# A hybrid encoder layer in Strassen–Winograd form: matrix memory's rows two tiles ahead, its weights behind the columns, and x's quarter in the fifth operand's buffer

## The chip, the cores and the metric

One core of one Trainium2 chip. The time is the device time of one execution in microseconds (us), and the median of several executions is compared. The span in a profile is the time from the first to the last instruction of one profiled execution.

## What is computed

One layer of a streaming encoder, all in float32: 2048 prompt tokens and 8 x 16 sample tokens, width 1024, so 17 tiles of 128 tokens (16 of the prompt, and the sample batch as tile 16). Four steps:

```python
z = x @ w_in                                  # queries, keys, values, gates, window heads
mix = concat(mlstm(z), window_attention(z))   # group A: 4 heads x 128; group B: 8 heads / 2 kv heads x 64
x = layer_norm(alpha * x + mix @ w_out)
x = layer_norm(alpha * x + (silu(conv(gate)) * conv(value)) @ w_down)   # gate, value: two halves of x @ w_up
```

Group A, the matrix memory, goes tile by tile. With b the running sum of the forget gates' logarithms over a tile, li the input gates', and C, n, m the state from the tile before:

```python
inter = b + m
dmat = where(causal, b[:, None] - b[None, :] + li[None, :], -inf)
mt = maximum(inter, max(dmat, -1))
w_inter = exp(inter - mt)
s = (q @ k.T) * exp(dmat - mt[:, None])
num = w_inter * (q @ C) + s @ v
```

num is divided by the larger of |den| and exp(-mt), normed by head, and C, n and m are carried to the next tile.

## The kernel before

**Phases.** Input projection (four blocks of up to five tiles, `IBLOCKS`), output projection, FFN up, FFN down. Each value is held as two parts, high and low, and each product is three matmuls. The projection works on pairs of halves with seven products instead of eight (Strassen–Winograd): in a block there are five groups g of weight columns, and for each the products s = 1, 7, 6, 2, 5, 3, 4. Their second operands are sums of quarters of x: `x_steps` casts each to high (ACT, L602) and subtracts to low (DVE, L603), into the buffers oh{s} and ol{s} that `x_slot(s)` gives. Beside the products stand direct tiles, ("t", block, tile, part), which multiply a tile of x with the gates' and keys' weights (PE L783). They use quarters of x of their own, hx[b, 1], hx[b, 2], hx[b, "b12"] and hx[b, 3]. So far "b12" lies in oh4/ol4, the fourth product's buffer.

**Banks.** The products of a group write three PSUM banks: A by s = 1 and 2; B by 6, 5 and 3; C by 7 and 4. `i_after` empties them: ACT copies B for s = 6 and 5 (L824 in groups 0 and 1 as scaled copies by `copy`, L816 for a whole bank A or B through `i_out`), DVE adds C to the copy (L828 and L830, for s = 5 and again for s = 4), and between groups ACT copies A to B (L852). A bank can be written again only when its reader is done.

**Order of the work.** PE's order is as the program writes it. `Chains.weave` steps three generators between the products: the sample batch, the matrix memory (`m_chain`) and windowed attention (`a_chain`). Each yields a cost, a delay in estimated time and a count of PSUM banks it needs. On the other engines a scheduler sets the order; `issue_after` holds an instruction behind another, and `behind_pe` holds a DMA behind PE's latest mark. All of the DMAs spoken of here are issued by SP, in SP's order, the weights' loads too: an SP row that waits holds the rows behind it.

**Weights.** A weight unit is loaded (wraw, L477), cast by ACT (L227), and split by DVE (w, L228). Of the input weights some products take sums that the kernel forms itself (txy, zt, and from DRAM zws).

**A tile of matrix memory.** `m_rows` (L1130) takes two transposes on PE (pgr, L1057 and L1058) and makes on DVE rows of 4 x 128: a scan for b (r_b, L1136), li - b (ay, L1137), a second scan for the running maximum (r_M, L1138), the negated row nmrow (L1140, L1141), a further row (L1068) and the carried m (L1144). `m_spread` step 0 writes nmrow to DRAM (zrow, L1150) and step 1 reads it back to all 128 partitions (nm, L1153). `m_tile` then makes columns (pcol on PE, col on DVE, L1079), dt = nm + mask (DVE L1175), emt (ACT L1084), wi = the inter-tile weights (ACT L1187, reads nm), dt's exponentials (ACT L1181), scores weighted by dt (sd, DVE L1198), kw (L1272), then pnum (PE L1282) and the state's update. `m_norm` norms (DVE L1216 to L1227), `m_scaled` makes ms and hn (DVE L1233, ACT L1235), `m_out` transposes hn (pht, PE L1245) and stores.

Before, `m_tile(t)` makes the rows of tile t + 1 right behind its own dt and spreads them in two later steps: step 0 before the scores, step 1 before pnum. So one row set is ahead.

Of the kernel before, what the change touches and what calls it, by code (L numbers as in the profile page):

```python
# [204 lines left out]
class Prog:  # L205
# [373 lines left out]
    def x_steps(self, b, *steps):  # L579

        nc, V = self.nc, self.nc.vector
        r = lambda q: self.xr[b, q]
        for s in steps:
            if s == "t3":
                self.spare = False
                self.xt = e = self.raw_slot([P, 4, HT]) if b else [self.tp.tile([P, 4, HT], F32, name="xt", tag="qk", bufs=2), False]
                V.tensor_sub(e[0], r(4), r(2))
            elif s == "t2":

                V.tensor_add(self.xt[0], self.xt[0], r(1))  # L590
            elif s == "t4":

                V.tensor_sub(r(4), r(3), self.xt[0])
                self.xt[1] = True
            elif s == "t1":

                V.tensor_sub(r(2), r(2), r(1))
            else:
                x = self.xt[0] if s in (7, 6) else r({1: 1, 2: 3, 3: 4, "b12": 2, 5: 2, 4: 4}[s])

                self.hx[b, s] = h, l = self.x_slot(4 if s == "b12" else s)
                nc.scalar.copy(h, x)  # L602
                V.tensor_sub(l, x, h.bitcast(F32))  # L603

# [17 lines left out]
    def i_dense(self):  # L622
# [18 lines left out]
        for q in (2, 4):  # L641
            for _ in range(2 + (q == 2) * 2):
# [15 lines left out]
                 ("t", 0, 0, -1): ["t2", 6], ("t", 0, 2, -1): ["t1", 5, "t4"]}  # L658
        self.sb, self.trans = {}, None

        passages = [{1: ["load"], 7: ["t3", 7], 6: ["t2", 6], 3: [3, "t4"], 4: ["b12", "t1"]},
                    {1: ["load"], 6: ["t3"], 7: [7, "t2"], 5: [6], 3: [3, "t4"], 4: ["b12", "t1"]}]
        sums = 0
        after = None
        for item in self.items:
# [49 lines left out]
            if g == last and b + 1 < nb:  # L715
                if s == 7:
                    self.rope_load(IBLOCKS[b + 1][2], 2)
                for x in passages[b > 0].get(s, ()):
                    if x == "load":
                        self.spare = True  # L720
                        self.x_load(b + 1, 1, 2, 3, 4)
                    else:
                        self.x_steps(b + 1, x)
            if (b, g, s) == (0, last, 4):
                self.x_steps(1, 1, 2)
                after = [6, 1]
            if g == last and b + 1 == nb and s in (7, 5, 2, 3):
                self.x_pair(0, (7, 5, 2, 3).index(s))
            with self.tc.issue_after(behind) if behind and b == 0 else nullcontext():
                self.advance()  # L730
                self.x_steps(0, *begin.get(item, ()))
                if item == ("p", 0, 0, 2):
                    self.x_single(4)
# [87 lines left out]
    def i_after(self, b, g, s):  # L821
# [15 lines left out]
            self.i_out(b, g, 0, 0, A)  # L837
        elif s == 5:
            u4 = self.zev()
            copy(u4, B)  # L840
            add(u4)
            self.i_out(b, g, 1, 1, u4)
        elif s == 4:
            add(self.u2)
            self.i_out(b, g, 1, 0, self.u2)
# [235 lines left out]

    def m_emt(self, col):
        emt = self.work("emt", [P, MH], bufs=2)
        self.nc.scalar.activation(emt, col[:, 36:40], AF.Exp)  # L1084
        return emt

    def place(self, t, blocks=IBLOCKS):
# [8 lines left out]
    def m_chain(self):  # L1096
# [3 lines left out]
        pend = None  # L1100
        self.rows = {}
        there = lambda t: t < NPT and self.i_done > self.place(t)[0]
        for t in range(NPT):
            while not there(t):
                yield 0, 500
            if pend is None:
                self.m_rows(t)
                self.m_spread(t, 0)
                self.m_spread(t, 1)
# [4 lines left out]
            hn = self.m_norm(*(yield from self.m_tile(t, *pend, *self.rows.pop(t))))  # L1114
            pend = None
            yield 950, 3000, 1
            self.m_scaled(hn)
            if there(t + 1):
                if t + 1 not in self.rows:
                    self.m_rows(t + 1)  # L1120
                    self.m_spread(t + 1, 0)
                    self.m_spread(t + 1, 1)
                pend = self.m_load(t + 1, *self.place(t + 1)),
            yield 150, 6800, 1
            self.m_out(t, hn[0])
            self.chains.done["m"] = t
        nc.sync.dma_start(self.a["m_p"], self.mc)
        nc.sync.dma_start(self.a["cn_p"], self.C)

    def m_rows(self, t):  # L1130
# [14 lines left out]
        self.rows[t] = [i, nm]  # L1145

    def m_spread(self, t, step):
        nc, z = self.nc, self.zrow[t]
        if step == 0:
            self.behind_pe(nc.sync.dma_start(z.rearrange("o (h m) -> (o h) m", h=MH), self.rows[t][1]))  # L1150
            return
        self.rows[t][1] = nm = self.work("nm", [P, MH, 129], bufs=2)
        self.behind_pe(nc.sync.dma_start(nm.rearrange("p h m -> p (h m)"), z.to_broadcast([P, MH * 129])))  # L1153

    def m_load(self, t, b, ti):
# [95 lines left out]
    def m_tile(self, t, load, i, nm):  # L1251
# [3 lines left out]
        col = self.m_cols(i)  # L1255
        with self.tc.issue_after(self.colcopy.ins):
            dt = self.m_masked(nm[:, :, :P], self.mcau)
        ahead = t + 1 < NPT and self.i_done > self.place(t + 1)[0]
        if ahead:
            self.m_rows(t + 1)  # L1260
        yield 330, 2800
        emt = self.m_emt(col)
        wi = self.m_inter(nm)
        self.m_exps(dt, col)
        yield 0, 5000, 2
        if ahead:
            self.m_spread(t + 1, 0)
        ps = self.m_scores(qk)
        kt = self.m_ktok(qk)
        sd = self.m_weighted(ps, dt)  # L1270
# [956 lines left out]
```

## Time and profile before

| | |
|---|---|
| median of 3 runs | 2307.58 us (2306.45 to 2310.1) |
| the profiled execution: its time | 2307.89 us |
| its span | 2305.7 us |
| PE, busy | 2266.6 us |
| DVE, busy | 1808.2 us |
| ACT, busy | 1306.8 us |
| POOL, busy | 225.5 us |

PE is TensorE's matmuls, PEld its weight loads, which overlap them; DVE is VectorE, ACT ScalarE, POOL GpSimd, SP SyncE (SPq where it issues a DMA). Times in views are us from the start of the span. A row of the timeline gives start, duration, engine, line, operation, written and read buffers, shapes, and in brackets how long the engine stood idle before it and what ended that. The input projection with matrix memory and attention between its products takes the first 870 us or so; the matrix memory's first prompt tile starts at about 280 us.

### The profile page before, as it was taken

The page shows a single profiled execution, that of the slowest core. Times are in us where ns is not written, and L with a number is a line of the kernel's source. Part 1 is how long each engine was busy: PE and PEld are TensorE (multiplying, and loading weights), DVE is VectorE, ACT ScalarE, POOL GpSimd, SP SyncE. Part 2 cuts the span into 40 slices and gives each one's busy share as a digit, 9 for nine tenths or more (in the row PEclk, how much of TensorE's full clock was granted, in tenths as well). Part 3 has the DMA queues.
Part 4 walks back from the last instruction along what each step waited for, and adds up shares of the span by engine and source line. Part 5 has one row for each costly group of instructions (what it writes and reads, how often), then busy time and mean ns, then how long its engine had stood idle before and what let it go on. Part 6 is the DMA issues. An engine that isn't in the chain of part 4 may idle for free.

```text
span 2305.7 us, 39752 instructions
## 1 busy us (share of the span) xinstructions
PE 2266.6 (98%) x14329; PEld 2086.1 (90%) x14329; DVE 1808.2 (78%) x3157; ACT 1306.8 (57%) x2465; POOL 225.5 (10%) x289
## 2 busy tenths in 40 slices
PE   8999999999999999999999999999999999999998
PEld 8999989898887778999999999999999988888887
DVE  8777686787789888987788666778766787796897
ACT  5453466676765665555556455555554644654753
POOL 0001001101122121200002000002000000000100
PEclk9999999999999999999999999999999999999999
DMA  7898999899986767787777889888998786656753
GB/s 279 299 322 287 297 308 328 295 303 332 320 278 237 241 220 248 282 322 282 275 270 263 282 309 322 308 305 270 328 292 260 240 286 225 240 196 225 242 188 110
DMA packets 299797, 629.23 MB, mean 273 GB/s; under 512 B 47373, under 2 KB 140625, under 8 KB 299601
## 3 DMA queue, kind: packets, MB, share of 16 engines
q1 hardware_dynamic: 298736, 623.55, 79.1%
q10 hardware_dynamic: 864, 3.15, 0.4%
q8 instruction: 113, 1.85, 0.3%
q14 instruction: 84, 0.68, 0.1%
HBM read 456.01 MB, written 170.59 MB: 272 GB/s over the span
## 4 chain that ended last, share of the span: by engine, by line
PE 78%; DVE 10%; DMA 6%; ACT 3%; issue 2%; SPq 0%; POOL 0%; DVEq 0%; ACTq 0%; POOLq 0%
PE dps L1931 18%; PE fup L1931 18%; PE dps L758 11%; PE dps L2135 6%; PE fht L2135 6%; PE fup L2135 5%; PE dps L232 2%; PE dps L233 2%; PE dps L234 2%; DMA txy<-wdn 2%; DVE w L228 2%; PE dps L783 1%; DMA w<-zws 1%; PE psx L767 1%; PE ppo L1420 1%
## 5 line engine op out<-in xcount | busy, mean ns | idle before, releaser
L1931 PE MATMUL dps<-hh,uw 128*128 128x384 f32 (+1 forms) x1848 | 477.5, 327 | 5.4 <-DVE u L1964 2.6
L1931 PE MATMUL fup<-hh,uw 128*128 128x384 f32 (+1 forms) x1848 | 476.4, 326 | 0.0
L1979 DVE SCALAR_TENSOR_TENSOR cc<-u,cw,cc 128x768 f32<-128x768 f32 (+1 forms) x264 | 257.7, 978 | 125.0 <-ACT cc L1977 121.6
L1931 PEld LDWEIGHTS dps<-hh,uw 128*128 128x128 f32 x1848 | 329.2, 188 | 7.9 <-DVE u L1964 3.2
L1931 PEld LDWEIGHTS fup<-hh,uw 128*128 128x128 f32 x1848 | 329.3, 188 | 0.0
L1931 PE MATMUL fup<-hl,uw 128*128 128x384 f32 (+1 forms) x924 | 301.3, 326 | 0.2 <-DVE hl L228 0.2
L1931 PE MATMUL dps<-hl,uw 128*128 128x384 f32 (+1 forms) x924 | 301.0, 326 | 0.0
L758 PE MATMUL dps<-w,oh 128*128 128x256 f32 x1344 | 252.1, 283 | 4.6 <-DMA w<-zws 2.2
L758 PEld LDWEIGHTS dps<-w,oh 128*128 128x128 f32 x1344 | 210.1, 188 | 17.1 <-issue 9.3
L228 DVE TENSOR_TENSOR w<-wraw,w 128x1024 fp32r<-128x1024 f32 (+1 forms) x155 | 185.8, 1202 | 50.4 <-ACT w L227 48.0
L227 ACT CAST uw<-wraw 128x1024 fp32r<-128x1024 f32 x126 | 123.2, 981 | 173.4 <-PE dps L2135 104.1
L227 ACT CAST w<-wraw 128x1024 fp32r<-128x1024 f32 (+1 forms) x155 | 155.0, 1005 | 88.9 <-PE dps L758 44.3
L228 DVE TENSOR_TENSOR uw<-wraw,uw 128x1024 fp32r<-128x1024 f32 x126 | 142.5, 1131 | 63.9 <-ACT uw L227 63.8
L758 PE MATMUL dps<-w,ol 128*128 128x256 f32 x672 | 187.2, 279 | 0.0
L1977 ACT ACTIVATE cc<-u,cw 128x768 f32<-128x768 f32 (+1 forms) x132 | 131.9, 1000 | 95.6 <-DVE u L1973 92.6
L758 PE MATMUL dps<-oh,w 128*128 128x256 f32 x896 | 167.0, 282 | 7.8 <-ACT zev L824 3.9
L1931 PEld LDWEIGHTS fup<-hl,uw 128*128 128x128 f32 x924 | 173.5, 188 | 1.1 <-DVE hl L228 1.1
L1931 PEld LDWEIGHTS dps<-hl,uw 128*128 128x128 f32 x924 | 173.5, 188 | 0.0
L2135 PE MATMUL fup<-uw,fu 128*128 128x512 f32 x726 | 169.3, 389 | 0.1
L2135 PEld LDWEIGHTS fup<-uw,fu 128*128 128x128 f32 x726 | 136.1, 188 | 28.7 <-ACT fht L2142 0.5
L2135 PE MATMUL dps<-uw,fu 128*128 128x512 f32 x660 | 160.9, 389 | 0.1
L758 PEld LDWEIGHTS dps<-oh,w 128*128 128x128 f32 x896 | 139.7, 188 | 14.1 <-ACT zev L824 4.5
(346 smaller groups left out, 4563.6 us busy)
## 6 DMA issues: line engine op xcount, KB each, us to landing
uw<-zw SPq DMA_DIRECT2D x176, 512.0 KB
zw<-uw SPq DMA_DIRECT2D x88, 512.0 KB
w<-zws SPq DMA_DIRECT2D x72, 512.0 KB
wv<-wup SPq DMA_DIRECT2D x66, 512.0 KB
wraw<-wi SPq DMA_DIRECT2D x62, 512.0 KB
wraw<-zt SPq DMA_DIRECT2D x60, 512.0 KB
wraw<-wdn SPq DMA_DIRECT2D x45, 512.0 KB
wraw<-wo SPq DMA_DIRECT2D x40, 512.0 KB
```

The lines of the kernel that those rows point to most:

```text
L227: nc.scalar.copy(hi, src)
L228: nc.vector.tensor_sub(lo, src, hi.bitcast(F32))
L232: mm(out, ah, bh, start=start, stop=False)
L233: mm(out, ah, bl, start=False, stop=False)
L234: self.mark = mm(out, al, bh, start=False, stop=stop)
L758: self.mark = mm(o, l, r, start=s in (1, 7) and c == k == i == 0, stop=k == 3 and i == 2, skip_group_check=True)
L767: mm(o, x[:, k], w[:, k], start=s == 1 and k == i == 0, stop=s in (2, 4) and k == 3 and i == 2, skip_group_check=True)
L783: mm(o, x, w, start=k == i == 0, stop=k == KD - 1 and i == 2, skip_group_check=True)
L1931: mm(ps, l[:, k], r[:, k], start=s in (1, 7) and k == 0 and i == 0, stop=k == 3 and i == 2, skip_group_check=True)
L1977: S.activation(c[:, v], u[:, v, 2:2 + n], AF.Identity, bias=w[3], scale=w[2])
L1979: V.scalar_tensor_tensor(c[:, v], u[:, v, i:i + n], w[i], c[:, v], op0=ALU.mult, op1=ALU.add)
L2135: mm(ps, l[:, k, c], r[:, k], start=s in (1, 4, 7) and u == 0 and k == 0 and i == 0, stop=u == nu - 1 and k == n - 1 and i == 2, skip_grou ...
```

## The change

Three things, in the diff below.

1. x's quarter "b12" goes to oh5/ol5 for blocks 1 to 3. For block 1 it is cast after product s = 5 of block 0's last group, behind the copy of bank B (`i_after` now returns that instruction), not after s = 4.
2. Matrix memory's rows: `m_tile(t)` no longer makes rows. Behind `m_scaled(t)` and the load of tile t + 1, the rows of tile t + 2 are made; step 0 of their spread follows `m_out(t)`; step 1 stands in `m_tile(t + 1)` behind its exponentials. A third entry in `self.rows` says whether step 1 has been issued. Where rows are missing, `at_once` makes them with both steps. Tile 0's and tile 1's rows are made this way: tile 0's when it starts, tile 1's behind `m_scaled(0)`. The first yield in `m_tile` goes from 330 to 180.
3. wi is issued behind emt.

```diff
-                self.hx[b, s] = h, l = self.x_slot(4 if s == "b12" else s)
+                self.hx[b, s] = h, l = self.x_slot((5 if b else 4) if s == "b12" else s)
...
-        passages = [{1: ["load"], 7: ["t3", 7], 6: ["t2", 6], 3: [3, "t4"], 4: ["b12", "t1"]},
+        passages = [{1: ["load"], 7: ["t3", 7], 6: ["t2", 6], 5: ["b12"], 3: [3, "t4"], 4: ["t1"]},
...
-                        self.x_steps(b + 1, x)
+                        with self.tc.issue_after(behind) if x == "b12" and s == 5 else nullcontext():
+                            self.x_steps(b + 1, x)
...
-            with self.tc.issue_after(behind) if behind and b == 0 else nullcontext():
+            with self.tc.issue_after(behind) if behind and b == 0 and s == 1 else nullcontext():
...
-            copy(u4, B)
+            done = copy(u4, B).ins
             add(u4)
             self.i_out(b, g, 1, 1, u4)
+            return done
...
-        self.nc.scalar.activation(emt, col[:, 36:40], AF.Exp)
+        self.emtcopy = self.nc.scalar.activation(emt, col[:, 36:40], AF.Exp)
...
+        def at_once(t):
+            if t not in self.rows:
+                self.m_rows(t)
+                self.m_spread(t, 0)
+                self.m_spread(t, 1)
...
             self.m_scaled(hn)
             if there(t + 1):
-                if t + 1 not in self.rows:
-                    self.m_rows(t + 1)
-                    self.m_spread(t + 1, 0)
-                    self.m_spread(t + 1, 1)
+                at_once(t + 1)
                 pend = self.m_load(t + 1, *self.place(t + 1)),
+            ahead = there(t + 2) and t + 2 not in self.rows
+            if ahead:
+                self.m_rows(t + 2)
             yield 150, 6800, 1
             self.m_out(t, hn[0])
+            if ahead:
+                self.m_spread(t + 2, 0)
...
-        ahead = t + 1 < NPT and self.i_done > self.place(t + 1)[0]
-        if ahead:
-            self.m_rows(t + 1)
-        yield 330, 2800
+        yield 180, 2800
         emt = self.m_emt(col)
-        wi = self.m_inter(nm)
+        with self.tc.issue_after(self.emtcopy.ins):
+            wi = self.m_inter(nm)
         self.m_exps(dt, col)
+        if t + 1 in self.rows and not self.rows[t + 1][2]:
+            self.m_spread(t + 1, 1)
         yield 0, 5000, 2
-        if ahead:
-            self.m_spread(t + 1, 0)
...
-        if ahead:
-            self.m_spread(t + 1, 1)
```

Lines of the changed kernel are 1 to 8 higher: L824 becomes L825, L828 and L830 become L829 and L831, L1079 becomes L1081, L1150 and L1153 become L1158 and L1161, L1175 becomes L1183, L1375 becomes L1379.

The instructions move at three places. First, ACT at the end of block 0's last group: the copy of bank B for s = 5 (L824), the gates' weights (128x2x264), the copy for s = 3 (L816), and the casts of x (L602). Before:

```order
L824 COPY zev<-dps 128x512
L227 CAST w<-wraw 128x2x264 x2
L816 COPY zev<-dps 128x512
L602 CAST oh<-xr 128x1024
L227 CAST w<-wraw 128x1024
L602 CAST oh<-xr 128x1024
L227 CAST w<-wraw 128x1024
```

Now:

```order
L825 COPY zev<-dps 128x512
L602 CAST oh<-xr 128x1024
L227 CAST w<-wraw 128x2x264 x2
L817 COPY zev<-dps 128x512
L602 CAST oh<-xr 128x1024
L227 CAST w<-wraw 128x1024 x2
```

The quarter's cast, before the last L602 of the piece, is now the first, ahead of three weight casts.

Second, DVE at the end of block 1's last group, where tile 0 of the matrix memory starts. Before (col, dt, the scan of tile 1's rows, the addition that empties bank C, and the subtraction of tile 1's rows):

```order
L1079 COPY col<-pcol 128x36
L1175 TENSOR_TENSOR dt<-nm,k_mcau 128x512
L1136 SCALAR_TENSOR_TENSOR r_b<-pgr,k_seg 4x128
L830 TENSOR_TENSOR zev<-dps,zev 128x512
L1137 TENSOR_TENSOR ay_765<-pgr,r_b 4x128
```

Now:

```order
L1081 COPY col<-pcol 128x36
L831 TENSOR_TENSOR zev<-dps,zev 128x512
L603 TENSOR_TENSOR ol<-xr,oh 128x1024
L1183 TENSOR_TENSOR dt<-nm,k_mcau 128x512
L228 TENSOR_TENSOR w<-wraw,w 128x1024
```

The addition has come ahead of dt, and tile 1's rows are gone from here.

Third, tile 1 of the matrix memory. SP before, from the write of tile 1's row (zrow_73) to its broadcast:

```order
L1150 DMA zrow_73<-nmrow 4x129
L929 DMA ropet<-rope 128x192
L1302 DMA kva<-zkv_161 128x256
L577 DMA xr<-xq 128x1024
L909 DMA zt<-txy 128x1024
L477 DMA wraw<-zws_2_94 128x1024
L477 DMA wraw<-wi 128x1024
L1153 DMA nm<-zrow_73 128x516
```

Now, with tile 0's output (zmix from mixm) and tile 2's row (zrow_74) behind it:

```order
L1158 DMA zrow_73<-nmrow 4x129
L910 DMA zt<-txy 128x1024
L477 DMA wraw<-wi 128x1024
L1161 DMA nm<-zrow_73 128x516
L477 DMA wraw<-zws_3_95 128x1024
L1247 DMA zmix_176<-mixm 128x4x128
L1158 DMA zrow_74<-nmrow 4x129
```

Two rows stand between the write and the broadcast where six stood, and both have moved behind the norm of tile 0. On DVE the same tile, before (the last addition of a group's bank C, a weight's split, col, dt and the scan of tile 2's rows):

```order
L1380 TENSOR_TENSOR aes<-k_sink,amx 128x4
L828 SCALAR_TENSOR_TENSOR zev<-dps,zev 128x512
L228 TENSOR_TENSOR w<-wraw,w 128x1024
L1079 COPY col<-pcol 128x36
L1175 TENSOR_TENSOR dt<-nm,k_mcau 128x512
L1136 SCALAR_TENSOR_TENSOR r_b<-pgr,k_seg 4x128
```

Now (L1379 are the four reductions of attention, two rows each, of which the first is shown):

```order
L228 TENSOR_TENSOR w<-wraw,w 128x1024
L1081 COPY col<-pcol 128x36
L1183 TENSOR_TENSOR dt<-nm,k_mcau 128x512
L1379 ISA sc,amx<-psc,k_mswa 128x256
L1379 ISA amx 128x1
...
L829 SCALAR_TENSOR_TENSOR zev<-dps,zev 128x512
L1383 SCALAR_TENSOR_TENSOR amx<-amx,nsink 128x4
L228 TENSOR_TENSOR w<-wraw,w 128x1024
```

dt, with the wait for nm, has come ahead of the four reductions and of the addition that empties bank C. The rows of tile 1 and of tile 2 stand further up, the scan, the subtraction and the second scan of tile 1 between the small instructions of tile 0's norm ahead of ms:

```order
L1231 TENSOR_TENSOR mr<-mr,emt 128x4
L1144 SCALAR_TENSOR_TENSOR r_b<-pgr,k_seg 4x128
L1232 RECIPROCAL mr<-mr 128x4
L906 TENSOR_TENSOR txy<-txy 128x512
L1233 TENSOR_TENSOR mq<-bmv,mr 128x4
L1145 TENSOR_TENSOR ay_765<-pgr,r_b 4x128
L1234 TENSOR_TENSOR mq<-mq,mr 128x4
L907 TENSOR_TENSOR txy<-txy 128x512
L1235 TENSOR_SCALAR mq<-mq 128x4
L1146 SCALAR_TENSOR_TENSOR r_M<-k_seg,mc,ay_765 4x128
L1241 TENSOR_TENSOR ms<-ms,mr 128x4
```

More of the change, by code (lines that the diff above doesn't have):

```diff
@@ L1106, in m_chain @@
             if pend is None:
-                self.m_rows(t)
-                self.m_spread(t, 0)
-                self.m_spread(t, 1)
+                at_once(t)
                 pend = self.m_load(t, *self.place(t)),
@@ L1113, in m_chain @@
                 yield 0, 1000, 2
-            hn = self.m_norm(*(yield from self.m_tile(t, *pend, *self.rows.pop(t))))
+            hn = self.m_norm(*(yield from self.m_tile(t, *pend, *self.rows.pop(t)[:2])))
             pend = None
@@ L1144, in m_rows @@
         V.tensor_add(self.mc, bc[:, P - 1:P], M[:, P - 1:P])
-        self.rows[t] = [i, nm]
+        self.rows[t] = [i, nm, False]
     def m_spread(self, t, step):
@@ L1151, in m_spread @@
             return
-        self.rows[t][1] = nm = self.work("nm", [P, MH, 129], bufs=2)
+        self.rows[t][1:] = nm, _ = self.work("nm", [P, MH, 129], bufs=2), True
         self.behind_pe(nc.sync.dma_start(nm.rearrange("p h m -> p (h m)"), z.to_broadcast([P, MH * 129])))
```

## The prediction, made before the result was seen

> **What bounds the kernel now.** I first read the page's table of busy times, then the busy time of the engines in three stretches of the span up to the two FFN halves (start and end; length; busy time of PE, PE's weight loads, DVE, ACT, POOL; granted clock; DMA share; GB/s).
>
> ```profile
> PE 2266.6 (98%) x14329; PEld 2086.1 (90%) x14329; DVE 1808.2 (78%) x3157; ACT 1306.8 (57%) x2465; POOL 225.5 (10%) x289
> 0.00:290.00 290.00, 279.22 (x2409) 270.15 (x2410) 215.04 (x347) 140.43 (x226) 13.73 (x17) 1.00 0.86 297
> 290.00:470.00 180.00, 169.47 (x1409) 156.78 (x1409) 137.38 (x399) 123.14 (x318) 16.82 (x17) 0.99 0.92 310
> 470.00:870.00 400.00, 396.32 (x2663) 329.24 (x2662) 328.37 (x931) 265.04 (x697) 72.72 (x56) 1.00 0.82 273
> ```
>
> PE is the bound: it works 2266.6 of 2305.7 us, so a change that leaves its matmuls alone can win at most the 39.1 us in which it stands. The edits act between about 145 and 870 us. From 290 to 470 (matrix memory's tiles 0 to 3) PE stands 10.5 us, from 470 to 870 only 3.7. Which waits those are, the view of waits tells (who waits for whom: total us, times, longest).
>
> ```profile
> PE dps L758 <- ACT zev L824: 4.4, 4, 2.5
> PE dps L783 <- DVE zev L830: 2.8, 2, 2.1
> PE dps L783 <- DVE ol L603: 2.7, 1, 2.7
> PE dps L758 <- DMA w<-zws: 2.2, 5, 0.8
> PE dps L758 <- ACT zev L816: 0.9, 1, 0.9
> PE pnum L1282 <- DVE sd L1198: 0.9, 1, 0.9
> PE pgr L1057 <- ACT pth L1415: 0.8, 1, 0.8
> PE pht L1245 <- ACT hn L1235: 1.7, 2, 1.0
> ```
>
> I then went to each in the timeline. The profiled execution took 2307.89 us, 2.2 more than its span; the median of the runs shown is 2307.58, so I sum against 2307.89 and take off 0.3 at the end.
>
> **The change part by part. x's quarter.** Timeline of ACT, DVE and PE before the first direct tile of block 1 (start, us, engine, line; in brackets the idle time before it and what ended it).
>
> ```profile
> 145.23 0.58 ACT L824 COPY zev<-dps 128x512 f32<-128x512 f32 x1
> 147.47 0.64 ACT L227 CAST w<-wraw 128x528 fp32r<-128x528 f32 x1 [0.51 <-DMA wraw<-wg]
> 151.53 1.05 ACT L227 CAST w<-wraw 128x1024 fp32r<-128x1024 f32 x1 [0.82 <-DMA wraw<-wi]
> 152.48 1.04 ACT L602 CAST oh<-xr 128x1024 fp32r<-128x1024 f32 x1
> 155.49 1.21 DVE L603 TENSOR_TENSOR ol<-xr,oh 128x1024 fp32r<-128x1024 f32 x1
> 153.57 0.39 PE L783 MATMUL dps<-w,oh 128*128 128x264 f32 x1 [0.28 <-ACT oh L602]
> 156.75 0.40 PE L783 MATMUL dps<-w,ol 128*128 128x264 f32 x1 [2.67 <-DVE ol L603]
> ```
>
> The quarter's cast stands behind a weight's cast that waits for its DMA, and behind the last product on the fourth operand. PE wants the quarter at about 153.3 and stands 0.28 for the high half and 2.67 for the low one. After the change the cast is the row behind the copy L824, which ends at 145.81. With its 1.04 and DVE's 1.21, behind at most one weight split, both halves are ready by about 149.3, four microseconds early. The move puts 1.04 us of ACT ahead of the gates' last weight cast at 147.47, which then ends at 149.2, four microseconds ahead of PE too: nothing new is late there, and PE's product hides it; without that cover it would cost its 1.04. Term: **-3.0**, with 0 and -3.0 as its ends, since what PE gains it may give to the next weights.
>
> **Rows of tile 1 no longer ahead of a column group's end.** Around tile 0 on DVE and PE:
>
> ```profile
> 289.54 0.68 DVE L1175 TENSOR_TENSOR dt<-nm,k_mcau 128x512 f32<-128x512 f32 x1
> 290.14 0.40 DVE L1136 TENSOR_TENSOR_SCAN r_b<-pgr,k_seg 4x128 f32<-4x128 f32 x1
> 290.47 0.65 DVE L830 TENSOR_TENSOR zev<-dps,zev 128x512 f32<-128x512 f32 x1
> 291.18 0.51 PE L783 MATMUL dps<-w,oh 128*128 128x264 f32 x2 [0.71 <-DVE zev L830]
> ```
>
> In the new order the addition stands straight behind col, with dt behind it and no scan: over 1 us earlier, so the 0.71 goes: **-0.7**. The scans of tile 1 go from this place, which is where DVE is short before sd: of the 0.9 that pnum waits I take **-0.5** (ends 0 and -0.9). The A copy's wait of 0.9 (L816, at 323) goes with the same backlog: **-0.9** (ends 0 and -0.9).
>
> **wi behind emt.** The largest wait left is 2.55 us at 327:
>
> ```profile
> 320.39 0.38 SPq L1153 DMA_DIRECT2D nm<-zrow  x1
> 325.97 1.28 ACT L1187 ACTIVATE wi<-nm 128x128 f32<-128x128 f32 x4 [2.87 <-DMA nm<-zrow]
> 327.16 1.03 ACT L227 CAST w<-wraw 128x1024 fp32r<-128x1024 f32 x1
> 328.33 1.28 ACT L1235 ACTIVATE hn<-hn,ms 128x128 f32<-128x128 f32 x4
> 329.52 0.58 ACT L824 ACTIVATE zev<-dps 128x512 f32<-128x512 f32 x1
> 330.14 0.39 PE L758 MATMUL dps<-oh,w 128*128 128x256 f32 x1 [2.55 <-ACT zev L824]
> ```
>
> wi of tile 1, which nobody needs yet, waits at the head of ACT for the broadcast, and the copy that frees a PE bank stands behind it. Behind emt it stands some 12 us later, so at this place ACT's 2.87 of idle and 1.28 of work go and the copy is done in time: **-2.5** (ends -1.3, where hn holds the copy, and -2.55).
>
> **The wait that is added.** Tile 1 is not two ahead. Its rows are made and spread at once when tile 0 is normed; only tiles 2 to 15 are made earlier. That moves nm of tile 1 from 320 to behind ms, and the consumer on DVE, dt, stands where it stood. The prices come from these rows: the seven DVE instructions of one row set at tile 0 (first and last), the SP pair, ms and the next consumers.
>
> ```profile
> 280.08 0.41 DVE L1136 TENSOR_TENSOR_SCAN r_b<-pgr,k_seg 4x128 f32<-4x128 f32 x1
> 282.08 0.14 DVE L1141 COPY nmrow<-mc 4x1 f32<-4x1 f32 x1
> 281.58 0.28 SPq L1150 DMA_DIRECT2D zrow<-nmrow  x1
> 284.78 0.32 SPq L1153 DMA_DIRECT2D nm<-zrow  x1
> 328.14 0.15 DVE L1233 TENSOR_TENSOR ms<-ms,mr 128x4 f32<-128x4 f32 x1
> 334.20 0.60 PE L1245 MATMUL pht<-ident,hn 128*128 128x128 f32 x4
> 336.56 0.41 DVE L1375 CUSTOM_DVE_ANT_0 sc<-psc,k_mswa 128x256 f32<-128x256 f32 x1
> ```
>
> From ms on: the row set interleaved with an addition and a weight split is done 2.8 us later; issue 0.3; landing up to 3.2 (281.58 to 284.78, SP standing meanwhile, with weight loads queued behind it); the broadcast 5.6 (320.39 to 325.97). So nm lands at ms + 11.9. Then dt (0.7 by the row at 289.54), four reductions of 0.41 that overlap (about 1.4 in all) and the addition L828 (0.6, as the one at 290.47), which in the new order all stand behind dt: the bank C is free at ms + 14.6. By the new PE order C is wanted 8.0 us of matmuls behind pht. The rows have pht 5.9 behind ms's end, of which 2.5 is the wait that goes, so 3.4: wanted at ms + 11.4, and PE stands 3.2 us. If pht follows as soon as hn is done (ms + 1.4), it is 5.2. I take **+3.5**, near the first; the ends are 0 (if ms comes early against PE) and +5.2. Queued behind the waiting dt on DVE are those reductions, the addition and a weight split; behind wi, which waits on ACT for the same nm, are dt's exponentials and a weight cast. PE waits for all of these.
>
> Whether the clock pays as well, one place shows:
>
> ```profile
> 457.00:462.40 5.40, 3.31 (x28) 3.10 (x27) 5.37 (x9) 5.40 (x16) 0.00 (x0) 1.00 0.94 269
> 462.40:466.00 3.60, 3.60 (x20) 3.60 (x19) 3.60 (x6) 2.70 (x9) 0.00 (x0) 0.53 1.04 333
> ```
>
> Behind the wait of 2.1 us there the granted clock was 0.53 for 3.6 us, which costs 1.7 us; behind the 2.67 and the 2.55 above I see no such stretch. One of three: an end of +1.7 for the range, not a term. (The Trainium skill, "TensorE: Matmul & The Clock Gate", section "What's actually happening", has the clock fall after an idle window of about 3.4 us; the drop behind 2.1 us disagrees. By that rule the new wait would cost nothing more below 3.4 us and 1.7 above.)
>
> **Tiles 2 to 15 and the rest.** The row sets are as many as before (16 of about 2.1 us of DVE, 280.08 to 282.22) and only stand elsewhere; their broadcasts start a tile earlier, so ACT no longer waits for nm. PE barely stood behind those waits: from 470 to 870 its whole idle time is 3.7. I take **-0.8**, the pgr row's wait (ends 0 and -2). The weights (2.2), the wait of 2.1 and its clock I leave: the addition there still stands behind tile 4's work on DVE.
>
> Sum: -3.0 - 0.7 - 0.5 - 0.9 - 2.5 - 0.8 + 3.5 = -4.9; 2307.89 - 4.9 - 0.3 = **2302.7**. The forecast's own range, with the ends of its terms, is 2299.5 to 2306.5.
>
> **Rivals.** *The new wait is hidden.* If zrow lands in under 1 us, or dt comes late on DVE anyway, the +3.5 goes: 2299.2. For it: ACT and DVE are each under 77% busy from 290 to 470. Against it: the SP pair above took 3.2 and 5.6 us, at a DMA share of 0.92. (The Trainium skill, "DMA: Bandwidth & Descriptors", section "Anatomy of one DMA — SWDGE (gpsimd) path", gives about 2.0 us plus bytes over 436 GB/s for a transfer. An estimate by it is 2.0 and 2.6 for this pair, 4.2 us under the rows, which would hide the wait; the rows disagree.) Chance 0.17.
>
> *x's gain is eaten by the weights behind it.* Block 1's first products follow at once.
>
> ```profile
> 161.58 1.23 DVE L228 TENSOR_TENSOR w<-wraw,w 128x1024 fp32r<-128x1024 f32 x1
> 167.77 0.39 PE L758 MATMUL dps<-oh,w 128*128 128x256 f32 x2
> ```
>
> The weights ready at 162.81 are used at 167.88, with PE 3 us earlier at 164.9: 2.1 us to spare, so this pair holds; but from 184 on products are fed at a DMA share near 0.9, and five waits for w<-zws show where none is spare. All of it lost: 2305.7. Chance 0.18.
>
> *The change does little:* tile 1 waits as long as it gains and x too is eaten, or the scheduler's order hides both: about 2307. Chance 0.05.
>
> *Slower: the rows stand ahead of ms.* In the new order the scan, the subtraction and the second scan of a row set stand on DVE between the norm's small instructions (the scan is 0.41 by its row; of the set's 2.1 I take 1.2 for these three), so ms, hn and pht come that much later at each of 14 tiles. It decides where pht follows hn on PE by less than 1.2 us; two places wait already (1.7 us). At tile 0 the slack is 4.6 (hn ends 329.6, pht starts 334.2). With ten tiles without slack it costs 12.0: 2314.7, and it takes eight or nine to be slower by over 0.2% than before. Chance 0.15.
>
> **How the numbers follow.** Forecast 0.45. About 0.2% (4.6 us) is what a measurement of this kernel can tell from no change, so faster is under 2303.0. The forecast lies on that line: 0.22 faster, 0.23 same. With the hidden wait (0.17), faster is 0.39 in all, rounded to 0.40. Same: 0.23, 0.18 for the eaten gain, 0.05 for little, less rounding 0.45. Slower 0.15. The range 2297 to 2311 takes in the hidden wait with 2 us more at tiles 2 to 15, the eaten gain, the clock's 1.7, and half of the slower case.
>
> **What would show it.** In the changed profile: the wait for ol L603 at 154 gone and the ACT cast of x before 148; no wait at 290 and 327; a wait of PE of some 3 us about 10 us behind the first pht, ended by the addition (now L829), with DVE's dt waiting for nm; no ACT wait for nm at tiles 2 to 15; the pht waits as they were. I am wrong if the pht waits grow, if waits for w<-zws grow by as much as x gained, or if PE's idle time from 470 to 870 moves by over 2 us.

## The result, and the profile after

The changed kernel took 2306.29 us, median of 22 runs (2299.81 to 2309.52), beside 2309.77 of the kernel before in 22 runs of the same sessions (2306.22 to 2320.71). The ratio is 0.9984, 95% interval 0.9978 to 0.9990: 3.7 us less, between 2.3 and 5.1. The forecast was a ratio of 0.9979, just inside that interval. The profiled execution has a span of 2303.8 us, 1.9 under that of before.

The same three stretches of the span in the changed kernel (columns as in the prediction):

```profile
0.00:290.00 290.00, 282.39 (x2435) 273.50 (x2436) 219.50 (x352) 142.59 (x230) 13.66 (x17) 1.00 0.86 300
290.00:470.00 180.00, 168.27 (x1401) 156.78 (x1400) 138.58 (x421) 120.06 (x320) 20.49 (x19) 0.98 0.92 314
470.00:870.00 400.00, 395.69 (x2656) 329.90 (x2655) 321.81 (x911) 265.04 (x694) 71.73 (x55) 1.00 0.81 272
```

PE has 3.2 us more work in the first 290 us: it stands less there, which is x's quarter. From 290 to 470 it stands 11.7 us, 1.2 more than before, and the granted clock is lower (0.98). The part on matrix memory has won nothing there. PE's waits in the whole of the changed kernel, those of the projection that answer to the rows of before, and the new ones:

```profile
PE dps L784 <- DVE zev L831: 4.7, 2, 4.4
PE dps L759 <- ACT zev L825: 2.5, 3, 1.5
PE pgr L1059 <- DVE C L1297: 1.7, 1, 1.7
PE dps L759 <- DVE zev L831: 1.7, 1, 1.7
PE dps L759 <- DMA w<-zws: 1.7, 3, 0.7
PE pnum L1286 <- DVE sd L1206: 1.3, 1, 1.3
PE dps L759 <- ACT dps L854: 1.3, 1, 1.3
PE ppt L1418 <- ACT pth L1419: 0.9, 1, 0.9
PE pht L1253 <- ACT hn L1243: 0.8, 1, 0.8
PE pht L1253 <- ACT pth L1419: 0.7, 1, 0.7
PE dps L759 <- ACT zev L817: 0.4, 1, 0.4
```

The wait of 2.7 for ol (L603 at the direct tile) is gone, and so is the one of 2.55 for a copy at 327. In their place are one of 4.4 for an addition (2.1 before), one of 1.7 for the pgr row, one of 1.5 for another copy (at 499), one of 1.3 for the bank's copy L854 and one of 0.9 for pth. The 1.7 for another addition, at 575, cannot be put down to the change: it was 0.85 in the first profile of the kernel before and 1.69 in its second one.

**x's quarter.** ACT, DVE and PE of the changed kernel before block 1's first direct tile:

```profile
145.00 0.58 ACT L825 COPY zev<-dps 128x512 f32<-128x512 f32 x1
145.48 1.05 ACT L602 CAST oh<-xr 128x1024 fp32r<-128x1024 f32 x1
147.37 0.63 ACT L227 CAST w<-wraw 128x528 fp32r<-128x528 f32 x1 [0.31 <-DMA wraw<-wg]
146.56 1.23 DVE L603 TENSOR_TENSOR ol<-xr,oh 128x1024 fp32r<-128x1024 f32 x1
152.84 0.41 PE L784 MATMUL dps<-w,oh 128*128 128x264 f32 x2
153.09 0.28 PE L784 MATMUL dps<-w,ol 128*128 128x264 f32 x1
```

Both halves are there at 147.8, five us before PE uses them, and the gates' last weights are cast at 148.0, when they were before. PE starts with the low half 0.25 us behind the high one. Counted by the same matmul in both traces, PE is 0.2 us ahead at 150 us and 3.7 ahead from 158 to 230.

**The end of block 2.** There PE is 3.9 us ahead at 451 us (by the matmul that starts at 451.0 in before) and 0.8 behind at 464. Not all of that is standing: counted from 100 us on, PE has done 12 more of the chains' matmuls than before at the first of these points and 24 more at the second. DVE and PE of the changed kernel, and the clock:

```profile
455.62 1.23 DVE L228 TENSOR_TENSOR w<-wraw,w 128x1024 fp32r<-128x1024 f32 x1
456.77 1.12 DVE L1297 SCALAR_TENSOR_TENSOR C<-C,wi,pcu 128x129 f32<-128x129 f32 x4
458.94 0.83 DVE L1230 SCALAR_TENSOR_TENSOR hn<-pnum,bmv,og 128x128 f32<-128x128 f32 x3
459.84 0.66 DVE L831 TENSOR_TENSOR zev<-dps,zev 128x512 f32<-128x512 f32 x1
455.92 0.28 PE L784 MATMUL dps<-w,ol 128*128 128x264 f32 x1
460.56 0.81 PE L784 MATMUL dps<-w,oh 128*128 128x264 f32 x2 [4.36 <-DVE zev L831]
```

```profile
456.00:460.70 4.70, 0.34 (x3) 0.14 (x1) 4.70 (x21) 2.79 (x8) 0.00 (x0) 0.90 0.90 283
460.70:464.00 3.30, 3.30 (x15) 3.30 (x16) 2.83 (x8) 1.64 (x4) 1.72 (x1) 0.50 0.99 302
464.00:468.00 4.00, 4.00 (x26) 4.00 (x25) 2.32 (x3) 1.82 (x4) 0.19 (x1) 0.67 1.00 360
```

The addition that empties bank C ends at 460.5, as it ended at 461.0 before, though PE needs it at 456.2. The state update and the norm of a matrix memory tile stand ahead of it on DVE; in the order of before they did not. The wait of 4.4 is followed by half clock from 459.8 to 466.6 us; the last of the three stretches takes in a part at full clock.

### The profile page after: what moved, and what is told of

Same layout as the page of the kernel before. It is cut to its first block, busy times and chain, and to the rows that moved or that the text cites. A ratio compares the mean times of both kernels' runs of the same rounds, so it can differ in the third digit from the quotient of the medians.

```text
span 2303.8 us, 39754 instructions
## 1 busy us (share of the span) xinstructions
PE 2265.1 (98%) x14329; PEld 2088.1 (91%) x14329; DVE 1804.9 (78%) x3157; ACT 1305.4 (57%) x2465; POOL 227.5 (10%) x289
## 3 DMA queue, kind: packets, MB, share of 16 engines
q8 instruction: 113, 1.85, 0.3%
## 4 chain that ended last, share of the span: by engine, by line
PE 82%; DVE 7%; DMA 5%; issue 3%; ACT 2%; POOL 0%; SPq 0%; DVEq 0%; ACTq 0%; POOLq 0%
PE dps L1935 19%; PE fup L1935 19%; PE dps L759 11%; PE dps L2139 6%; PE fht L2139 6%; PE fup L2139 5%; PE dps L232 2%; PE dps L233 2%; PE dps L234 2%; DVE w L228 1%; PE dps L784 1%; PE ppo L1424 1%; DMA w<-zws 1%; PE psx L768 1%; PE psc L1375 1%
```

## The experiments

A ratio is to the runs of the kernel before on the same chip, with its interval; in us, times 2310. PE's idle time is given in two pieces of work, cut at the same matmuls in every trace: those that start at 140, 285 and 880 us in before, so that the pieces hold the same projection work, and all of the matrix memory's work is done at the last cut. It is the length of the piece less PE's busy time. Each profile is of one execution, and those of x alone and of the change with the sums later are of the fastest of their 12 runs, so the idle times go with the profile and not with the median. The rows for the second piece (length; busy of PE, PE's weight loads, DVE, ACT and POOL; clock; DMA share; GB/s) of before, of the change, of x alone and of the rows without the hold on wi:

```profile
285.06:880.05 594.99, 580.78 (x4153) 498.85 (x4152) 478.52 (x1350) 395.06 (x1026) 92.43 (x75) 1.00 0.85 285
```

```profile
281.23:877.46 596.23, 579.84 (x4153) 500.72 (x4152) 472.45 (x1348) 392.95 (x1025) 92.93 (x75) 0.99 0.84 285
```

```profile
280.70:873.29 592.59, 580.89 (x4153) 499.56 (x4153) 476.48 (x1348) 395.30 (x1027) 92.09 (x75) 1.00 0.85 286
```

```profile
281.21:887.99 606.78, 581.71 (x4153) 500.85 (x4152) 471.87 (x1348) 393.99 (x1027) 90.43 (x74) 0.99 0.83 280
```

| kernel | ratio to before | us | idle, first piece | idle, second piece | its length |
|---|---|---|---|---|---|
| before; again | 1 | 0 | 4.2; 3.6 | 14.2; 14.5 | 595.0; 596.6 |
| the change; again | 0.9984 (0.9978 to 0.9990) | -3.7 | 1.2; 1.6 | 16.4; 17.6 | 596.2; 599.2 |
| x alone | 0.9977 (0.9967 to 0.9988) | -5.3 | 0.3 | 11.7 | 592.6 |
| rows and wi | 1.0015 (1.0006 to 1.0024) | +3.5 | 3.8 | 20.4 | 603.2 |
| wi alone | 1.0005 (0.9994 to 1.0016) | +1.2 | 3.5 | 14.4 | 597.4 |
| x and wi | 0.9983 (0.9971 to 0.9995) | -3.9 | 0.8 | 14.9 | 597.5 |
| the change, tile 1 ahead | 0.9988 (0.9977 to 0.9999) | -2.8 | 0.4 | 16.8 | 597.4 |
| the change, chains held | 0.9994 (0.9982 to 1.0006) | -1.4 | 0.6 | 17.2 | 596.7 |
| the change, sums later | 0.9983 (0.9973 to 0.9993) | -3.9 | 0.7 | 13.1 | 593.4 |
| x alone, sums later | 0.9969 (0.9958 to 0.9981) | -7.2 | 0.8 | 11.2 | 591.2 |
| x and rows, no hold | 1.0032 (1.0018 to 1.0046) | +7.4 | 1.1 | 25.1 | 606.8 |
| x alone, chains held | 0.9985 (0.9974 to 0.9996) | -3.5 | 0.7 | 17.6 | 600.5 |

**x's quarter alone**, on the kernel before (the lines on `done` and on `s == 1` in the diff of the change belong to it):

```diff
-                self.hx[b, s] = h, l = self.x_slot(4 if s == "b12" else s)
+                self.hx[b, s] = h, l = self.x_slot((5 if b else 4) if s == "b12" else s)
...
-        passages = [{1: ["load"], 7: ["t3", 7], 6: ["t2", 6], 3: [3, "t4"], 4: ["b12", "t1"]},
+        passages = [{1: ["load"], 7: ["t3", 7], 6: ["t2", 6], 5: ["b12"], 3: [3, "t4"], 4: ["t1"]},
...
-                        self.x_steps(b + 1, x)
+                        with self.tc.issue_after(behind) if x == "b12" and s == 5 else nullcontext():
+                            self.x_steps(b + 1, x)
```

> The kernel before with x's quarter moved, and nothing else of the change. Theory 1 (the parts add up; x's move is nearly the whole gain, and what it wins stays): 3.0 to 3.7 us faster than before, PE's direct tile of block 1 starts its low half without the 2.67 us wait, and PE is still 3 us or more ahead of the kernel before at 470 us. Theory 2 (the addition on DVE at the end of block 2 takes what PE gains ahead of it, from wherever it comes): PE is 3.7 us ahead at 290 us, its wait for the addition at about 458 us grows from 2.1 to 4 us or more, and less than 1.5 us is left at 470 us and in the time.

Measured: 5.3 us faster (2.8 to 7.6). The wait of 2.67 is gone, PE is 4.5 us ahead at 305 us, 5.4 at 461 and 6.9 at 470, since the wait at the end of block 2 is here 1.7 and no half clock follows it (the one piece at half clock stands at 353, behind a wait of 1.9). Theory 2 falls: the end of block 2 does not take a gain by itself.

**Rows and wi without x's quarter**: the changed kernel with the lines of the diff above taken back:

```diff
-                self.hx[b, s] = h, l = self.x_slot((5 if b else 4) if s == "b12" else s)
+                self.hx[b, s] = h, l = self.x_slot(4 if s == "b12" else s)
```

> The change with x's quarter left as it was before: rows two ahead and weights behind the columns alone. Theory 1 (parts add up): the wait of 2.55 us at 327 us goes, but new waits of 1.3 us for sd, 1.7 us for the pgr bank and 0.7 us for pht replace it: within 1 us of before. My own sum for this part was 1.9 us faster. Theory 2 (the end of block 2 takes it): the time is the same as before within 1 us as well, but then with PE 2 us or more ahead of before at 450 us.

Measured: 3.5 us slower (1.4 to 5.5). Theory 1 had the direction of each wait, not the sum; my own sum, 1.9 us faster, had the wrong sign. The wait at the end of block 2 is 4.9 here, there are new ones of 1.9 for pht and 1.7 for sd, and four stretches at half clock where before shows one; one of the four stands behind the wait for x's quarter, which the rows do not touch.

**wi behind emt alone**:

```diff
-        wi = self.m_inter(nm)
+        with self.tc.issue_after(self.emtcopy.ins):
+            wi = self.m_inter(nm)
```

> The kernel before with the weights wi issued behind emt, and nothing else. Theory 1: the ACT wait of 2.87 us for nm at 326 us and PE's 2.55 us at 327 us go, no new wait for the pgr bank or for sd comes, since the rows stay where they were: 2 to 2.5 us faster. Theory 2: PE is 2.5 us ahead at 350 us and at most 1 us ahead at 470 us; the time is within 1 us of before.

Measured: 1.2 us slower (1.4 faster to 3.7 slower), so no gain of 2 us. The trace tells why. ACT, DVE and PE of this kernel at the place where before waited for nm:

```profile
330.01 1.28 ACT L1235 ACTIVATE hn<-hn,ms 128x128 f32<-128x128 f32 x4 [4.85 <-DVE ms L1233]
331.19 0.57 ACT L824 ACTIVATE zev<-dps 128x512 f32<-128x512 f32 x1
329.21 0.69 DVE L903 TENSOR_TENSOR txy<-txy 128x512 f32<-128x512 f32 x1 [2.86 <-DMA txy<-wdn]
329.82 0.15 DVE L1233 TENSOR_TENSOR ms<-ms,mr 128x4 f32<-128x4 f32 x1
331.82 0.58 PE L758 MATMUL dps<-oh,w 128*128 128x256 f32 x1 [3.12 <-ACT zev L824]
```

wi has gone from ACT's head, and hn stands there and waits for ms, 4.85 us. ms stands on DVE behind a sum of the FFN's down weights that waits for its load. PE's wait for that copy is 3.12, where it was 2.55. ACT's waits, before and with wi held, say it for the whole span:

```profile
ACT hn L1235 <- DVE ms L1233: 23.9, 12, 3.8
ACT wi L1187 <- DMA nm<-zrow: 22.4, 8, 5.1
```

```profile
ACT hn L1235 <- DVE ms L1233: 43.4, 16, 5.0
```

22.4 us of waiting for nm went, 19.5 us of waiting for ms came.

**x's quarter and wi**, without the rows: the kernel before with the two diffs above (x's quarter alone, wi alone).

> The kernel before with x's quarter moved and wi behind emt; the rows stay one tile ahead. Theory 1: the sum of the two single ones, 5 to 6 us faster than before and 1.5 to 2.5 us faster than the changed kernel, if the two-ahead rows are what costs. Theory 2: PE is 6 us ahead at 350 us and loses 4 us or more of it at the end of block 2; about as the changed kernel, 2 to 4 us faster than before.

Measured: 3.9 us faster (1.2 to 6.7); the sum of the single ones was -4.1. Beside the change (-3.7) nothing is gained by leaving the rows out, and x alone is not beaten. The time is inside theory 2's bounds, but not for its reason: PE is 0.3 ahead at 350 us and loses nothing at the end of block 2. Both theories took wi's 2.5 for real.

**Tile 1 two ahead as well**, in the changed kernel:

```diff
                 at_once(t)
+                if t == 0:
+                    self.m_rows(1)
+                    self.m_spread(1, 0)
```

> The changed kernel, with tile 1's rows made and their first spread issued when tile 0 starts, so that tile 1 too is two ahead. Theory A (what the rows cost is the place of tile 1's work: it shifts the chain of tiles so that tile 3's state update and norm stand on DVE ahead of the addition at the end of block 2): the waits for the pgr bank at 319 us (1.7) and of DVE for nm at 334 us (1.05) go, the wait at 456 us falls from 4.5 to 2 us or less, and the time is 3 to 6 us under the changed kernel's, about that of x's move alone. Theory B (the rows two ahead cost a little at every tile, by pht and pgr waits of 1 to 2 us spread over blocks 2 and 3): within 1.5 us of the changed kernel.

Measured: 2.8 us faster than before (0.2 to 5.3), no better than the change. The waits at 319 and 334 are gone, and the one at the end of block 2 fell from 4.4 to 2.4; PE is 11 us ahead of before at 470 us. But it is 3.0 ahead at 630. In block 3 come waits of 1.2 for the bank's copy and 2.5 for an addition, half clock behind it, and 1.9 for pth. Theory A had the waits right, and the time wrong. The lead at 470 is not work of the chains put off: PE has done as many of their matmuls there as in before (786 each, from 100 us on). It goes in the waits: over the work that before does from 470 to 630 us (1328 matmuls in both), PE stands 7.3 us of 168.0, where it stood 1.7 of 160.0.

**Chains held in block 2's last product**, in the changed kernel:

```diff
-            self.chains.hold = item[0] == "t" and item[1] > 0
+            self.chains.hold = item[0] == "t" and item[1] > 0 or item == ("p", 2, last, 4)
```

> The changed kernel, with the chains of matrix memory and attention held during the last product of block 2, as they are already during the direct tiles behind it. Nothing else changes. Theory A: tile 3's state update and norm then stand behind the addition on DVE; PE's wait at 456 us falls from 4.5 to 1.5 us or less, the granted clock stays at 1.00 behind it, and the time is 3 to 5 us under the changed kernel's. Theory B: that wait falls as well, but what is held comes back as waits at the start of block 3, and the time stays within 1.5 us of the changed kernel's.

Measured: 1.4 us faster than before (1.4 slower to 4.2 faster). The wait fell to 1.8 and the clock stayed at 1.00 there. PE is 9.6 us ahead at 470, 2.6 at 630, and waits of 2.2 for a copy and 1.8 for pth are new. That is theory B's answer: what is held (23 of the chains' matmuls at 470 us, beside the changed kernel) comes back. The time is 2.3 us above the change's, inside the intervals.

**The down weights' sums one step later**, in the changed kernel:

```diff
-                steps = (6, 2, 5) if g == last - 1 else (6, 5, 3)
+                steps = (6, 2, 5) if g == last - 1 else (6, 3, 4)
```

> The changed kernel, with the sums of the FFN's down weights (txy) in blocks 2 and 3 made behind product 3 and stored behind product 4, where they were made behind 5 and stored behind 3 (the last but one group left as it is). They are off PE's path, but each first sum waits on DVE for its load. Theory C (in blocks 2 and 3 it is these waits at the head of DVE, 2 to 4 us each, that hold ms, sd and the additions, and the wait for nm on ACT was only hidden behind them): DVE's waits for txy from wdn fall by half or more, and the time is 2 to 5 us under the changed kernel's. Against it (theory A or B): those waits fall, but PE's waits stay where they are, and the time is within 1.5 us.

Measured: 3.9 us faster than before, as the change. DVE's waits for these loads fell from 11.5 to 7.7 us, a third, and PE's waits stayed. So they are not what limits the changed kernel, as far as this took them away.

**The same with x's quarter alone**: the kernel before with the diff of x's quarter and this one of the sums.

> The kernel before with x's quarter moved, as in the run of that part alone, and with the sums of the FFN's down weights made behind product 3 and stored behind product 4. Theory C: PE's waits of 1.9 us at 322 and 2.1 us at 350 us go, and with them a stretch at half clock: 3 to 6 us under x's move alone. Against it: within 1.5 us of x's move alone.

Measured, in 7 runs: 7.2 us faster than before (4.4 to 9.7), the fastest of all; beside x alone 1.9 us, inside the intervals. PE's waits at 322 and 350 are still 1.9 and 1.7, so theory C is not borne out. This version's interval (0.9958 to 0.9981) just overlaps that of the change (0.9978 to 0.9990).

**x's quarter and the rows, without the hold on wi**:

```diff
-        with self.tc.issue_after(self.emtcopy.ins):
-            wi = self.m_inter(nm)
+        wi = self.m_inter(nm)
```

> The changed kernel with wi no longer held behind emt: x's quarter and the rows two ahead alone. If the hold on wi is what takes back part of x's gain, this is 1.5 to 3 us under the changed kernel, about x's move alone (5 us under before). If the rows are, it is the changed kernel's time within 1.5 us, with the wait for the pgr bank at 319 us and the wait of 4 us or more at the end of block 2 still there.

Measured, in 6 runs: 7.4 us slower than before (4.1 to 10.6), 11 slower than the change. I expected one of two small numbers. Two ahead does not take the wait for nm from ACT: it is 17.6 us in 9 waits again (22.4 in 8 before), and PE waits 5.5 us in four places for the bank's copy L854. Of that 2.6 stands behind hn, which waits for ms 3.3 us:

```profile
392.54 1.28 ACT L1243 ACTIVATE hn<-hn,ms 128x128 f32<-128x128 f32 x4 [3.27 <-DVE ms L1241]
396.73 0.61 ACT L854 COPY dps<-dps 128x512 f32<-128x512 f32 x1
```

But the changed kernel has the same wait of hn (3.27 us, at 389), and PE waits only 1.26 for the copy there, so these rows do not show what the missing hold costs. By the times, the hold wins nothing that these runs can show with rows one ahead, and is needed with rows two ahead; by which waits stays open.

**x's quarter alone, chains held in block 2's last product**: the kernel before with the diff of x's quarter and the one of the held chains.

> x's quarter moved, nothing else of the change, and the chains held during the last product of block 2. If the wait at the end of block 2 (1.9 us at 454 in the run of x alone) is due to the chains' work on DVE ahead of the addition, it falls under 1 us and the time is 1 to 3 us under x alone. If what is held comes back in block 3, as it did when the chains were held in the changed kernel, PE is ahead at 470 us and no longer at 630 us, and the time is within 1.5 us of x alone.

Measured: 3.5 us faster than before, 1.8 less than x alone (inside the intervals). The wait at 454 fell from 1.9 to 0.4 (by the matmuls' spacing: from start to start, less the usual 0.12 us); PE was 8.2 us ahead at 470, 5.4 at 630, and 2.1 behind at 880. So the first reading had the wait right and the time wrong, and the lead comes back as the second says, but later: at 630 it was still there, and the time is just outside its 1.5 us.

**Both kernels once more**, with no edit. First the kernel before:

> The kernel before once more, for a second profile. If a given wait sets the clock, the same waits come back within 0.3 us and the granted clock falls to about 0.5 at 462 us again and nowhere else. If it is chance which of the waits of about 2 us and more is followed by a stretch at half clock, the waits come back and the stretch stands elsewhere, or at another number of places; two executions then differ by about 1.7 us for each stretch.

Measured: the waits come back, at 153 (2.7), 327 (2.7) and 459 (3.1, it was 2.3, by the matmuls' spacing). Half clock came at three places, where the first profile has one. The second profile of before, around the first two:

```profile
149.00:155.00 6.00, 4.22 (x37) 4.01 (x35) 4.58 (x5) 5.03 (x6) 0.00 (x0) 1.00 0.94 315
155.00:160.00 5.00, 4.29 (x22) 4.29 (x23) 3.89 (x4) 1.05 (x1) 0.00 (x0) 0.66 0.87 273
325.00:330.00 5.00, 2.47 (x23) 2.27 (x20) 2.62 (x6) 4.10 (x11) 1.02 (x1) 0.98 1.04 391
330.00:334.00 4.00, 4.00 (x20) 3.75 (x22) 3.79 (x6) 2.40 (x5) 0.00 (x0) 0.60 0.86 228
```

In the first profile these four stretches all have 1.00. Two more stretches at 1.7 us each should make this execution 3.4 us longer; its span is 2.0 longer.

Then the changed kernel:

> The changed kernel once more, for a second profile. The wait at the end of block 2 comes back with 4 us or more, since the order on DVE sets it; the wait for the pgr bank at 319 us with 1.5 us or more; PE's waits for tile 1's nm behind the first pht stay under 0.5 us. Half clock behind the wait at the end of block 2 in any case, since it is longer than 3.4 us; elsewhere by chance.

Measured: a span of 2309.4, 5.6 over the first profile. The wait at the end of block 2 is 5.4 by the matmuls' spacing (4.5 in the first), the pgr wait 2.0; at 499 a wait of 1.65 has become 2.8 with half clock behind it. The order is the same, so that much differs from one execution to the next.

## Why the prediction was right, point by point

The time and its direction came out as forecast; the sum did so by errors that cancel, which is luck: x's quarter won more than its term, and the part on matrix memory, forecast as a gain, was a loss when measured alone. The range of 2299.5 to 2306.5 is also not what the ends of the terms give: added up, they give 2297.5 to 2310.8, or 2312.5 with the clock's 1.7. By its steps:

- **x's quarter, -3.0:** right. The wait went, and the idle time of the first piece fell from 4.2 to 1.2. x alone gives -5.3 in the runs (2.8 to 7.6), more than forecast: PE arrives earlier in block 2 and stands 2.5 less in the second piece too. The rival that block 1's weights eat the gain did not happen: PE keeps its 3.7 to 230 us, and the waits for w<-zws are 1.7 in all (2.2 before).
- **The addition at 290, -0.7:** right in kind, half in size. It now stands straight behind col, and the wait there fell from 0.88 to 0.52 by the matmuls' spacing.
- **sd, -0.5, and the A copy, -0.9:** sd went the other way, 0.9 to 1.3; the copy's wait fell from 0.9 to 0.4.
- **wi behind emt, -2.5:** this step failed. I took the wait named at ACT's head for the cause, and set hn's hold only as an end at -1.3. The row that refutes it stood in the prediction: ms starts at 328.14 and hn at 328.33, so hn could not have run sooner, and the copy behind hn neither. With wi gone the copy ran no sooner, and PE's wait for it was 3.1 instead of 2.5. Two waits lay over each other, and the one that ends last was not the one that the view names.
- **Tile 1's wait for nm, +3.5:** the mechanism is there and the size was off; the rival that it is hidden held, though not by a landing under 1 us. In the changed kernel nm lands 8.7 us behind ms's end (325.89), not 11.9:

```profile
325.73 0.16 DVE L1241 TENSOR_TENSOR ms<-ms,mr 128x4 f32<-128x4 f32 x1 [0.85 <-POOL ms L1236]
326.98 0.32 SPq L1158 DMA_DIRECT2D zrow<-nmrow  x1
329.31 0.32 SPq L1161 DMA_DIRECT2D nm<-zrow  x1
334.68 0.69 DVE L1183 TENSOR_TENSOR dt<-nm,k_mcau 128x512 f32<-128x512 f32 x1 [1.05 <-DMA nm<-zrow]
336.67 0.69 DVE L829 SCALAR_TENSOR_TENSOR zev<-dps,zev 128x512 f32<-128x512 f32 x1
```

  The row was written from 1.1 us behind ms on, not 3.1, because the scans stood ahead of ms; it landed in 2.3 us, not 3.2, and the broadcast took 5.3. The prediction's estimate of 2.0 and 2.6 for this pair goes by a section on transfers that GpSimd issues, while SP issues these. DVE stood 1.05 for nm, and PE did not stand for the addition.
- **Tiles 2 to 15, -0.8, and the end of block 2 left as it was:** this failed too. The pgr wait of 0.8 at 624 went, waits of 0.9 at 361, 1.3 at 394 and 1.5 at 499 came, and the end of block 2 went from 2.1 to 4.4 with a second piece of half clock. That rows two ahead end ACT's wait for nm was wrong too: without the hold on wi 17.6 us of it are left. The pgr wait at 319 I had not seen: `at_once(1)` and the rows of tile 2 ask for a bank twice in a row, and the second waits for DVE's state update, which stands behind a sum that waits 1.5 us for its load. It was gone with tile 1 ahead.

```profile
317.67 0.69 DVE L905 TENSOR_TENSOR txy<-txy 128x512 f32<-128x512 f32 x1 [1.54 <-DMA txy<-wdn]
318.55 1.11 DVE L1297 SCALAR_TENSOR_TENSOR C<-C,wi,pcu 128x129 f32<-128x129 f32 x4
```

- **The slower rival, rows ahead of ms:** not so. Tile 0's ms waits for POOL's power anyway (0.85 in its row above), and the scans lie in that time; the two pht waits are 0.8 and 0.7 (1.7 in all before).

For the matrix memory's part the forecast was -1.9; measured alone it is +3.5 (1.4 to 5.5). Beside x alone it costs the change 1.6 us (-3.7 where x alone has -5.3), which is inside the intervals. Where it loses is shown for single waits; that they add up to the loss is not shown. Two edits cut down the largest, at the end of block 2 (from 4.4 to 2.4 and 1.8), and the time did not follow. What sets how far PE can run ahead of the chains in block 3 stays open.

## What to carry to other kernels

Before taking away a wait at the head of a queue, look at what the next instruction in that queue waited for: hn's start 0.2 us behind ms was the sign that nothing would be won. What can win is the wait with nothing behind it: x's quarter stood behind a buffer still being read and an unrelated load, PE waited for it alone, and another buffer was all the gain that these runs show. A kernel whose chains share PE with dense work is compared at a point where the chains are done, not in between: with x alone a lead of 6.9 us at 470 us was still there at 880, but leads of 8 to 11 us at 470, in the three kernels with tile 1 ahead or the chains held, were worth 3 or less at 880. The changed kernel was 3.3 us behind at 400 us with 35 more of the chains' matmuls done, and 2.6 ahead at 880.

## What the runs showed of the hardware

Behind a wait of PE the granted clock fell to 0.5 in pieces of 3.41 us, which cost up to 1.7 us each. Over the fourteen profiles, from 100 to 880 us, the length of the wait alone does not say where: of 33 waits of 1.3 to 1.75 us (by the matmuls' spacing) one was followed by such a piece, of 33 of 1.75 to 2.45 us 9 were, and of 17 over 2.5 us 15 were, four of them by two pieces in a row (6.83 us).

Where the wait lies in time does say it. In each trace all changes of the clock lie whole multiples of 3.413 us apart. Cut into windows on that grid, PE stood 1.79 us or more (by the timeline's idle times) in the window ahead of 25 of the 26 falls, and 1.40 ahead of the other; in the 3145 windows at full clock with no fall behind them it stood at most 1.85. A window at half clock was followed by another in the four cases in which PE stood 0.65 us or more in it, and by full clock where it stood 0.50 or less. So the same wait at 327 was followed by half clock in one execution of the kernel before and not in the other: here is the window in which most of it lies, and the next one, in the first profile and then in the second. PE stood 1.85 us in the one and 2.42 in the other.

```profile
326.04:329.45 3.41, 1.56 (x14) 1.36 (x12) 1.92 (x4) 3.26 (x9) 0.30 (x1) 1.00 1.03 401
329.45:332.87 3.42, 2.73 (x20) 2.32 (x22) 3.30 (x7) 3.20 (x7) 0.00 (x0) 1.00 0.84 257
```

```profile
326.37:329.78 3.41, 0.99 (x9) 0.79 (x7) 2.40 (x4) 3.41 (x10) 0.00 (x0) 1.00 1.04 394
329.78:333.20 3.42, 3.31 (x15) 3.31 (x16) 3.38 (x7) 2.62 (x6) 0.00 (x0) 0.50 0.82 231
```

The Trainium skill, "TensorE: Matmul & The Clock Gate", section "What's actually happening", states a fall after at least one idle window of about 3.4 us and calls the window free-running. The grid and the length of a piece agree with that window; that a window a little over half idle was enough does not agree with the stated minimum. Where the grid lies differs from one execution to the next, so with two to four waits of about 2 us and more in a kernel, single executions differ by several us for that reason alone, and an effect of 2 us needs some tens of runs, or the idle time between fixed matmuls.
